# First norm of a two-layer decoder trunk: input read transposed by k-tiles instead of transposed on TensorE

## Chip, cores and metric

The kernel runs on one core of one Trainium2 chip. The metric is the device time of one execution in microseconds (us). Matrix products are made by TensorE (PE in the profile; PEld is its weight load), elementwise work by VectorE (DVE), ScalarE (ACT) and GpSimd (POOL). SyncE (SP) issues most of the loads.

## The reference, cut to what matters

One sequence of 256 tokens with 1024 features goes through two layers (an attention mixer and a SwiGLU block each) and a last norm. The change concerns the norm at the very start and the input projection of the even layer behind it:

```python
def rmsnorm(x, g):
    xf = x.astype(jnp.float32)
    y = xf * lax.rsqrt(jnp.mean(xf * xf, axis=-1, keepdims=True) + NORM_EPS)
    return (y * g.astype(jnp.float32)).astype(x.dtype)
...
    for layer in range(DEPTH):
        j = layer // 2
        h = rmsnorm(x, norm_mix[layer])
        if layer % 2 == 0:
            y = h @ ev_w_in[j]
            qa_nope, qa_rope, c_kv, ka_rope, iq, ik, iw, qb, kb, vb = split_cols(y, EVEN_SPLITS)
...
        x = x + mix
        x = x + swiglu(rmsnorm(x, norm_ffn[layer]), ffn_w_gate[layer], ffn_w_up[layer], ffn_w_down[layer])
    return rmsnorm(x, norm_final)
```

## The kernel before

**Tiling.** The 256 tokens are two tiles `t` of 128. The 1024 features are eight k-tiles of 128 (`KD = 8`). A product contracts over features, so its stationary operand must have features on partitions and tokens along the columns; x lies in memory with tokens first. The kernel therefore transposes x on TensorE: `first_half(nm, t, h)` takes four k-tiles (`h` is the half of the features) of one token tile, multiplies by the identity `ident` into a PSUM bank `pt_x` (L294), and scales by the gain, which is read as a column per k-tile (`gc0`).

**Split into two parts.** Each product is made of three: every operand is split into a high part (`hi`, rounded by a ScalarE copy) and a low part (`lo`, the difference, by VectorE), and `mm3` adds hi x hi, hi x lo and lo x hi (L332, L333, L334). The activations live in one wide tile `aW` (`Norm.wide`) with k-tile, part and token.

**The factor of the norm comes later.** The sum of squares isn't needed for the products. `Norm.square` makes it on ScalarE from natural x, `rsqrt_sum` adds eps on VectorE and raises to the power -0.5 on GpSimd (L226, L227) into `rs[t]`, which multiplies the results of the projection (in `rope`, L392 and after).

**Weights.** The class `Weights` streams all weights in the order of their use: `load` issues a tile (SP queue, L95), `prepare` splits it (`w_hi` on ScalarE, L110; `w_lo` on VectorE, L113), `next` hands it out and prepares six tiles ahead. A tile of the input projection holds two k-tiles of one chunk of columns; the chunks are `EV_CHUNKS` (328, 416, 384, ...), four tiles each. `project` works through one chunk: 4 tiles x 2 k-tiles x 2 token tiles x 3 = 48 products. What this text calls the first chunk has 328 columns, the second 416.

**Order.** The program is written with a tile framework. Its scheduler sets the order of each engine's instructions when the kernel is built, and each engine then runs its list in that order and waits where a semaphore says so. SP's loads and what is marked `pin` keep the order of the code. The start is: seven dummy products (`WARM`, L193) without any input; identity and gain column on ScalarE's queue; halves of x and weight tiles in turns on SP's queue; then the rest of the constants (`con`), `small`, and more weights. `even_mixer` multiplies the first chunk's result by `rs` and the rope tables, transposes it (`pt_i`) and goes on to index scores (`ps_i`). Natural x (`xs`) is needed again at the first residual, at the end of the even mixer.

Of the kernel before, what the change touches and what calls it, by code (L numbers as in the profile page):

```python
# [7 lines left out]
F32 = mybir.dt.float32  # L8
# [7 lines left out]
D = 1024  # L16
# [10 lines left out]
WARM = 7  # L27
# [47 lines left out]
class Weights:  # L75
# [15 lines left out]
    def load(self, upto):  # L91
        while len(self.raw) < min(upto, len(self.queue)):
            src, kk, w = self.queue[len(self.raw)]
            raw = self.spare(len(self.raw)) or self.rpool.tile([P, WCOLS], F32, tag="raw", bufs=self.bufs[0], name="w_raw")
            self.tc.keep_in_program_order(self.tc.nc.sync.dma_start(raw[:, : kk * w], src))  # L95
            self.raw.append(raw)

    def prepare(self, upto, behind=False):

        nc = self.tc.nc  # L100
        while len(self.ready) < min(upto, len(self.queue)):
# [8 lines left out]
            act = nc.scalar.activation(hi[:, :n], raw[:, :n], AF.Copy)  # L110
            if behind:
                self.tc.keep_in_program_order(act)
            nc.vector.tensor_sub(lo[:, :n], raw[:, :n], hi[:, :n])  # L113
# [11 lines left out]
def trunk(tc, x, w0, w1, sm0, cw, vec, gcol, cst, out, dbg=None):  # L125
# [58 lines left out]
    A.dma_start(con[:, :P], cst[:, :P])  # L184
    gc0 = base.tile([P, KD], F32, tag="gc0", name="gc0")
    A.dma_start(gc0, gcol)

# [11 lines left out]
    load_x(0, 0)  # L199
    W.load(1)  # L200
    load_x(1, 0)
    W.load(2)
    load_x(0, 1)
    load_x(1, 1)
    W.load(4)
    pin(nc.sync.dma_start(con[:, P:], cst[:, P:]))
# [83 lines left out]
    def first_half(nm, t, h):  # L290

        pt = t_bank("pt_x").rearrange("p (k c) -> p k c", k=4)
        for i in range(4):
            TE.transpose(pt[:, i], xs[t][:, (4 * h + i) * P : (4 * h + i + 1) * P], ident)  # L294
        hi, lo = nm.aT[t]
        if t == 0 and h == 0:
            for k in range(4):
                g = gc0[:, k : k + 1]
                pin(A.activation(hi[:, k], pt[:, k], AF.Copy, scale=g))
                V.scalar_tensor_tensor(lo[:, k], pt[:, k], g, hi[:, k], op0=ALU.mult, op1=ALU.subtract)  # L300
        else:
            xg = nat("xg").rearrange("p (k c) -> p k c", k=4)
            V.tensor_mul(xg, pt, gc0[:, 4 * h : 4 * h + 4].unsqueeze(2).broadcast_to([P, 4, P]))
            split(hi[:, 4 * h : 4 * h + 4], lo[:, 4 * h : 4 * h + 4], xg)
# [156 lines left out]
    def even_mixer(nm, goff):  # L461
        aT, rs = nm.aT, nm.rs
        with tc.tile_pool(name="even", bufs=1, side="left", reuse_waits="tile") as pool:
# [52 lines left out]
            tc.keep_in_program_order(nc.sync.dma_start(sm, sm0))  # L516
            for t in range(NT):
# [427 lines left out]
    for h in range(2):  # L945
        for t in range(NT):
            first_half(first, t, h)
            W.prepare(2 * h + t + 1, behind=(h,t)==(0,1))
    for t in range(NT):
        for h in range(2):  # L950
            first.square(t, h)
# [135 lines left out]
```

## Time and profile before

| | |
|---|---|
| median of 3 runs | 658.24 us (657.57 to 660.4) |
| profiled execution | 659.6 us |
| its span, first to last instruction | 657.8 us |
| instructions | 10005 |
| PE busy | 643.6 us (98%) |
| VectorE / ScalarE / GpSimd busy | 488.4 / 396.7 / 13.0 us |
| DMA | 109.15 MB, mean 166 GB/s |

Times in the rows are us from the start of the span, where not marked ns. A row of the timeline has start, duration, engine, line, operation, what is written and read, the count, and in brackets idle time ahead of it with what ended it. A row of a group has the count, then the busy time in us, the mean ns of one, and idle time with its releasers. A row of loads has the queue, the count, KB each and the us from issue to landing. PE's rows overlap, since products are pipelined: the distance between two starts is the pace, not the duration.

### The profile page before, as it was taken

The numbers are of one execution on the slowest core, as the hardware profiler recorded it, in microseconds if no ns is written. First come the engines' busy times: TensorE is split into PE (matmuls) and PEld (weight loads), VectorE is DVE, ScalarE is ACT, GpSimd is POOL, SyncE is SP. The second block draws the span as 40 slices with busy tenths as digits, with TensorE's granted clock in tenths as the row PEclk, the third lists the DMA queues.
The fourth block names the chain that finished last, engine by engine and source line by source line (L and its number), as shares of the span: only waits on it lengthen the run. The fifth ranks groups of instructions, "written<-read, shape, count | busy, mean of one in ns | idle before, by whom it ended". The sixth has DMA issues, their size and how long they took to land.

```text
span 657.8 us, 10005 instructions
## 1 busy us (share of the span) xinstructions
PE 643.6 (98%) x3512; PEld 538.5 (82%) x3512; DVE 488.4 (74%) x1115; ACT 396.7 (60%) x800; POOL 13.0 (2%) x26
## 2 busy tenths in 40 slices
PE   8999999999999999999999999999999999999995
PEld 5978888788888888888888877776888888888884
DVE  5999976758977777644579889896698787875424
ACT  5785748548655555433367599695586555554312
POOL 1000000100000000000000000000000000000000
PEclk9999999999999999999999999999999999999999
DMA  8845355138866655664098312410387555555501
GB/s 290 287 138 160 97 166 156 32 111 272 251 193 177 188 184 193 190 192 144 8 344 293 131 65 96 161 65 1 129 271 233 195 184 190 186 190 190 194 25 65
DMA packets 31729, 109.15 MB, mean 166 GB/s; under 512 B 3648, under 2 KB 3904, under 8 KB 31424
## 3 DMA queue, kind: packets, MB, share of 16 engines
q1 hardware_dynamic: 31104, 107.92, 49.6%
q8 instruction: 28, 0.46, 0.3%
q10 hardware_dynamic: 576, 0.59, 0.3%
q14 instruction: 21, 0.17, 0.1%
HBM read 107.46 MB, written 1.05 MB: 165 GB/s over the span
## 4 chain that ended last, share of the span: by engine, by line
PE 84%; ACT 6%; DVE 4%; DMA 4%; issue 2%; POOL 1%; SPq 0%; POOLq 0%; ACTq 0%
PE ps_u L439 12%; PE ps_g L439 11%; PE ps_out L332 7%; PE ps_out L334 7%; PE ps_out L333 7%; PE ps_u L440 6%; PE ps_g L440 6%; PE ps_in L332 5%; PE ps_in L334 5%; PE ps_in L333 5%; DMA w_raw<-in_w 2%; PE ps_o L936 2%; PE pt_p L920 2%; ACT w_hi L110 2%; PE ps_s L901 2%
## 5 line engine op out<-in xcount | busy, mean ns | idle before, releaser
L113 DVE TENSOR_TENSOR w_lo<-w_raw,w_hi 128x1024 fp32r<-128x1024 f32 (+5 forms) x200 | 234.7, 1180 | 93.3 <-ACT w_hi L110 90.9
L110 ACT ACTIVATE w_hi<-w_raw 128x1024 fp32r<-128x1024 f32 (+5 forms) x200 | 203.7, 1023 | 132.1 <-PE ps_out L334 56.8
L439 PE MATMUL ps_u<-aW,w_hi 128*128 128x512 f32 x352 | 124.6, 396 | 0.4 <-DVE hn L452 0.4
L439 PE MATMUL ps_g<-aW,w_hi 128*128 128x512 f32 x352 | 124.5, 395 | 0.3 <-DVE aW L243 0.3
L440 PE MATMUL ps_u<-aW,w_lo 128*128 128x256 f32 x352 | 98.7, 280 | 0.0
L440 PE MATMUL ps_g<-aW,w_lo 128*128 128x256 f32 x352 | 98.7, 280 | 0.0
L439 PEld LDWEIGHTS ps_g<-aW,w_hi 128*128 128x128 f32 x352 | 66.0, 187 | 16.3 <-DVE aW L243 0.9
L439 PEld LDWEIGHTS ps_u<-aW,w_hi 128*128 128x128 f32 x352 | 66.0, 187 | 16.0 <-DVE hn L452 0.7
L332 PE MATMUL ps_in<-w_hi,aW 128*128 128x512 f32 (+5 forms) x208 | 77.3, 372 | 0.6 <-ACT aW L242 0.5
L333 PE MATMUL ps_in<-w_lo,aW 128*128 128x512 f32 (+5 forms) x208 | 77.4, 372 | 0.1
L334 PE MATMUL ps_in<-w_hi,aW 128*128 128x512 f32 (+5 forms) x208 | 75.8, 365 | 0.0
L333 PE MATMUL ps_out<-w_lo,hT_hi 128*128 128x512 f32 x176 | 68.6, 390 | 0.0
L334 PE MATMUL ps_out<-w_hi,hT_lo 128*128 128x512 f32 x176 | 68.6, 390 | 0.0
L332 PE MATMUL ps_out<-w_hi,hT_hi 128*128 128x512 f32 x176 | 68.6, 390 | 0.0
L440 PEld LDWEIGHTS ps_g<-aW,w_lo 128*128 128x128 f32 x352 | 66.5, 189 | 0.0
L440 PEld LDWEIGHTS ps_u<-aW,w_lo 128*128 128x128 f32 x352 | 66.5, 189 | 0.0
L402 ACT ACTIVATE e<-e,bias 128x128 f32<-128x128 f32 (+1 forms) x96 | 42.4, 445 | 2.4 <-DVE bias L401 2.4
L332 PEld LDWEIGHTS ps_in<-w_hi,aW 128*128 128x128 f32 x208 | 39.7, 191 | 5.0 <-ACT aW L242 0.7
L334 PEld LDWEIGHTS ps_in<-w_hi,aW 128*128 128x128 f32 x208 | 39.5, 190 | 4.7 <-issue 0.5
L333 PEld LDWEIGHTS ps_in<-w_lo,aW 128*128 128x128 f32 x208 | 39.5, 190 | 4.4 <-issue 0.5
L334 PEld LDWEIGHTS ps_out<-w_hi,hT_lo 128*128 128x128 f32 x176 | 33.0, 188 | 6.9
L332 PEld LDWEIGHTS ps_out<-w_hi,hT_hi 128*128 128x128 f32 x176 | 33.0, 188 | 6.9
(225 smaller groups left out, 886.6 us busy)
## 6 DMA issues: line engine op xcount, KB each, us to landing
w_raw<-in_w SPq DMA_DIRECT2D x176, 512.0 KB, 4.2
w_raw<-in_w SPq DMA_DIRECT2D x8, 384.0 KB, 4.9
gain<-in_vec SPq DMA_DIRECT2D x4, 512.0 KB, 4.3
cw<-in_cw SPq DMA_DIRECT2D x2, 1024.0 KB, 8.1
w_raw<-in_w SPq DMA_DIRECT2D x4, 416.0 KB, 5.0
w_raw<-in_w SPq DMA_DIRECT2D x4, 328.0 KB, 5.7
w_raw<-in_w SPq DMA_DIRECT2D x4, 304.0 KB, 2.7
x<-in_x SPq DMA_DIRECT2D x4, 256.0 KB, 5.7
```

The source lines that it names most:

```text
L110: act = nc.scalar.activation(hi[:, :n], raw[:, :n], AF.Copy)
L113: nc.vector.tensor_sub(lo[:, :n], raw[:, :n], hi[:, :n])
L332: TE.matmul(ps, act[0][:, k], wh, start=start, stop=False)
L333: TE.matmul(ps, act[0][:, k], wl, start=False, stop=False)
L334: TE.matmul(ps, act[1][:, k], wh, start=False, stop=stop)
L402: A.activation(e, e, AF.Exp, scale=-1.0, bias=bias, accum_out=den)
L439: TE.matmul(dst[f], wh[:, i, c], wide[:, k].rearrange("p z q -> p (z q)"), start=k == 0, stop=False)
L440: TE.matmul(dst[f][:, :T], wl[:, i, c], wide[:, k, 0], start=False, stop=k == KD - 1)
L901: mmi = TE.matmul(sb[:, i], qS[t][:, h], kz[:, par, :, :ns], start=z == 0, stop=z == 1)
L920: TE.transpose(pt[:, i, b, st], e[:, i, b, st * P : (st + 1) * P], ident)
L936: pin(TE.matmul(ob[64 * par : 64 * par + 64], vv[:, st, c : c + 64], pTs[par][:, b, st].rearrange("p j c -> p (j c)"), start=False, stop=l ...
```

## The change

The host passes x a second time, as `xt`: partition p holds, for each k-tile, feature p of it for all 256 tokens. Four tiles `xT` take two k-tiles each. `first_pair` makes the high and low parts straight from them (k-tile by k-tile, 256 tokens wide), so `first_half`, its transposes and the early load of the identity go. The sum over features is now one over partitions: `first_square` squares each `xT` on ScalarE into scratch (the place of natural x, which isn't loaded yet), GpSimd adds the four results, `first_scale` adds the last two halves and sums over partitions by a product with a column of ones, one per token tile (`ps_ms`); eps and power follow as before. The first xT tile and the first weight tile are loaded in two parts each and split in two parts. Natural x is loaded in `even_mixer` behind `sm0`, `con` in one piece behind the first weights, and `WARM` is 9.

```diff
-WARM = 7
+WARM = 9
...
-    def load(self, upto):
+    def load(self, upto, between=None):
...
-            self.tc.keep_in_program_order(self.tc.nc.sync.dma_start(raw[:, : kk * w], src))
+            parts = kk if not self.raw else 1
+            for j in range(parts):
+                c = slice(j * kk * w // parts, (j + 1) * kk * w // parts)
+                self.tc.keep_in_program_order(self.tc.nc.sync.dma_start(raw[:, c], src[:, c]))
+                if between and j == 0:
+                    between()
...
-            act = nc.scalar.activation(hi[:, :n], raw[:, :n], AF.Copy)
-            if behind:
-                self.tc.keep_in_program_order(act)
-            nc.vector.tensor_sub(lo[:, :n], raw[:, :n], hi[:, :n])
+            parts = kk if i == 0 else 1
+            for j in range(parts):
+                c = slice(j * n // parts, (j + 1) * n // parts)
+                nc.scalar.activation(hi[:, c], raw[:, c], AF.Copy)
+                nc.vector.tensor_sub(lo[:, c], raw[:, c], hi[:, c])
...
-    A.dma_start(con[:, :P], cst[:, :P])
     gc0 = base.tile([P, KD], F32, tag="gc0", name="gc0")
     A.dma_start(gc0, gcol)
+    one = base.tile([P, 1], F32, tag="one", name="one")
+    V.memset(one, 1.0)
...
-    load_x(0, 0)
-    W.load(1)
-    load_x(1, 0)
-    W.load(2)
-    load_x(0, 1)
-    load_x(1, 1)
-    W.load(4)
-    pin(nc.sync.dma_start(con[:, P:], cst[:, P:]))
+    xT = [nat("xT") for _ in range(KD // 2)]
+
+    def load_xT(p, i):
+        pin(nc.sync.dma_start(xT[p][:, i.start * T : i.stop * T], xt[:, (2 * p + i.start) * T : (2 * p + i.stop) * T]))
+
+    load_xT(0, slice(0, 1))
+    W.load(1, between=lambda: load_xT(0, slice(1, 2)))
+    for p in range(1, KD // 2):
+        load_xT(p, slice(0, 2))
+        W.load(p + 1)
+    pin(nc.sync.dma_start(con, cst))
...
-    def first_half(nm, t, h):
...
+    def first_pair(nm, p):
+
+        for i in range(2):
+            k = 2 * p + i
+            g = gc0[:, k : k + 1]
+            src = xT[p][:, i * T : (i + 1) * T]
+            A.activation(nm.wide[:, k, 0], src, AF.Copy, scale=g)
+            V.scalar_tensor_tensor(nm.wide[:, k, 1], src, g, nm.wide[:, k, 0], op0=ALU.mult, op1=ALU.subtract)
+
+    sums = xs[1][:, :512]
+
+    def first_square(p):
+
+        dst = sums if p == 0 else xs[0][:, 512 * (p % 2) : 512 * (p % 2) + 512]
+        A.activation(dst, xT[p], AF.Square, scale=1.0 / math.sqrt(D))
+        if p:
+            G.tensor_tensor(sums, sums, dst, op=ALU.add)
+
+    def first_scale(nm):
+
+        G.tensor_tensor(sums[:, :T], sums[:, :T], sums[:, T:], op=ALU.add)
+        pm = t_bank("ps_ms")
+        for t in range(NT):
+            TE.matmul(pm[:, t : t + 1], sums[:, t * P : (t + 1) * P], one, start=True, stop=True)
+        for t in range(NT):
+            V.tensor_scalar(nm.rs[t], pm[:, t : t + 1], EPS, None, op0=ALU.add)
+            G.tensor_tensor(nm.rs[t], nm.rs[t], half_pow[:, :1], op=ALU.pow)
...
             tc.keep_in_program_order(nc.sync.dma_start(sm, sm0))
+            for h in range(2):
+                for t in range(NT):
+                    load_x(t, h)
...
-    for h in range(2):
-        for t in range(NT):
-            first_half(first, t, h)
-            W.prepare(2 * h + t + 1, behind=(h,t)==(0,1))
-    for t in range(NT):
-        for h in range(2):
-            first.square(t, h)
+    for p in range(KD // 2):
+        first_pair(first, p)
+        W.prepare(p + 1)
+        if p:
+            first_square(p - 1)
+    first_square(KD // 2 - 1)
+    first_scale(first)
...
+    xt = x.reshape(T, KD, P).transpose(2, 1, 0).reshape(P, KD * T)
```

What the scheduler makes of it stands in the order of each engine. On TensorE before, from the last dummy product on, transposes of x (`pt_x`) stand among the products of the first chunk (`ps_in_208` and `ps_in_209` are its two token tiles):

```order
L193 MATMUL warm_ps_85<-warm_83 128x512
L294 MATMUL pt_x_110<-con_75,x0_73 128x128 x4
L294 MATMUL pt_x_127<-con_75,x1_74 128x128 x4
L332 MATMUL ps_in_208<-w_hi_123,aW_107 128x328
L333 MATMUL ps_in_208<-w_lo_124,aW_107 128x328
L334 MATMUL ps_in_208<-w_hi_123,aW_107 128x328
```

On TensorE now the dummies are followed directly by products. Near the end of the first chunk (token tiles `ps_in_196` and `ps_in_197`, fourth weight tile `w_hi_152`, `w_lo_153`) the two sum products stand behind the fourth of the twelve products of that tile; the second chunk begins with `ps_in_312` and `ps_in_313`:

```order
L354 MATMUL ps_in_196<-w_hi_152,aW_116 128x328
L355 MATMUL ps_in_196<-w_lo_153,aW_116 128x328
L356 MATMUL ps_in_196<-w_hi_152,aW_116 128x328
L354 MATMUL ps_in_197<-w_hi_152,aW_116 128x328
L323 MATMUL ps_ms_161<-one_82,x1_74 128x1 x2
L355 MATMUL ps_in_197<-w_lo_153,aW_116 128x328
...
L354 MATMUL ps_in_312<-w_hi_200,aW_116 128x416
L354 MATMUL ps_in_313<-w_hi_200,aW_116 128x416
L355 MATMUL ps_in_312<-w_lo_201,aW_116 128x416
```

The transposes are gone from TensorE's list, and eight products of the first chunk now stand behind the sum products. On VectorE before, from the eps of the first norm to the low parts of the second chunk's weight tiles (128x832):

```order
L226 TENSOR_SCALAR rs<-ms_166 128x1
L226 TENSOR_SCALAR rs<-ms_173 128x1
L477 TENSOR_TENSOR lam_p<-small 128x128
L483 TENSOR_SCALAR subg<-small 128x128
L478 TENSOR_REDUCE lam_185<-lam_p 128x2
L243 TENSOR_TENSOR aW<-xg,aW 128x4x128
L392 SCALAR_TENSOR_TENSOR n_294<-ps_in,rs,con 128x320
L481 TENSOR_SCALAR nlam<-lam_185 128x1
L113 TENSOR_TENSOR w_lo<-w_raw,w_hi 128x832 x3
L394 SCALAR_TENSOR_TENSOR rope_b<-ps_in,rs,con 128x5x32
```

and the same place on VectorE now:

```order
L499 TENSOR_TENSOR lam_p<-small 128x128
L325 TENSOR_SCALAR rs<-ps_ms 128x1 x2
L500 TENSOR_REDUCE lam_173<-lam_p 128x2
L505 TENSOR_SCALAR subg<-small 128x128
L414 SCALAR_TENSOR_TENSOR n_282<-ps_in,rs,con 128x320
L503 TENSOR_SCALAR nlam<-lam_173 128x1
L416 SCALAR_TENSOR_TENSOR rope_b<-ps_in,rs,con 128x5x32 x2
L527 TENSOR_SCALAR wv<-ps_in,rs 128x8
L119 TENSOR_TENSOR w_lo<-w_raw,w_hi 128x832
L419 TENSOR_TENSOR n_282<-n_282,rope_b 128x320
```

The two half ropes and `wv` now stand ahead of the first low part of the second chunk, and the next low part comes after the rope's sum; before, three low parts came first. On ScalarE the exponent of lambda (L501, which waits for VectorE's L500) now stands ahead of all four high parts of the second chunk, where before one of them was ahead of it. From the middle of the even layer's input projection on, past the attention scores' first products, the lists of all engines read alike but for the line numbers.

More of the change, by code (lines that the diff above doesn't have):

```diff
@@ L94, in load, with prepare @@
             raw = self.spare(len(self.raw)) or self.rpool.tile([P, WCOLS], F32, tag="raw", bufs=self.bufs[0], name="w_raw")
-            self.tc.keep_in_program_order(self.tc.nc.sync.dma_start(raw[:, : kk * w], src))
+            parts = kk if not self.raw else 1
[4 more added lines that the diff above has]
+                    between()
             self.raw.append(raw)
-    def prepare(self, upto, behind=False):
+    def prepare(self, upto):
         nc = self.tc.nc
@@ L122, in next, with trunk @@
         return got
-def trunk(tc, x, w0, w1, sm0, cw, vec, gcol, cst, out, dbg=None):
+def trunk(tc, x, xt, w0, w1, sm0, cw, vec, gcol, cst, out, dbg=None):
     nc = tc.nc
@@ L288, in square @@
                 rsqrt_sum(self.rs[t], ms)
-    def first_half(nm, t, h):
[L292 to L304, printed above, removed]
+    def first_pair(nm, p):
[19 more added lines that the diff above has]
+            G.tensor_tensor(nm.rs[t], nm.rs[t], half_pow[:, :1], op=ALU.pow)
     class Final:
@@ L1067, in host_layout @@
     gcol = i["norm_mix"][0].reshape(KD, P).T
-    return {"x": i["x"].reshape(T, D), "w0": w0, "w1": w1, "sm0": sm0, "cw": cw, "vec": vec, "gcol": gcol, "cst": constants()}
+    x = i["x"].reshape(T, D)
+    xt = x.reshape(T, KD, P).transpose(2, 1, 0).reshape(P, KD * T)
+    return {"x": x, "xt": xt, "w0": w0, "w1": w1, "sm0": sm0, "cw": cw, "vec": vec, "gcol": gcol, "cst": constants()}
 def kernel(**inputs):
```

## The prediction

> **What bounds the kernel now.** I read the page's chain first (who sets the end), then the windows by stage (span, PE busy, PE weight load, VectorE, ScalarE, GpSimd, clock, DMA share, GB/s), then the timeline of the first 29 us.
>
> ```profile
> PE 84%; ACT 6%; DVE 4%; DMA 4%; issue 2%; POOL 1%; SPq 0%; POOLq 0%; ACTq 0%
> ...
> 7.00:19.00 12.00, 11.49 (x62) 10.38 (x63) 9.87 (x23) 9.75 (x22) 1.60 (x2) 1.00 0.92 323
> 19.00:28.40 9.40, 9.40 (x54) 9.25 (x54) 9.03 (x19) 5.47 (x9) 0.00 (x0) 1.00 0.85 261
> 28.40:46.00 17.60, 17.41 (x91) 13.80 (x90) 16.30 (x51) 15.06 (x31) 1.14 (x2) 1.00 0.65 228
> 46.00:58.00 12.00, 11.97 (x75) 11.51 (x74) 11.83 (x44) 8.15 (x13) 0.00 (x0) 1.00 0.23 66
> 58.00:131.00 73.00, 72.30 (x410) 59.60 (x408) 59.62 (x180) 47.28 (x121) 2.03 (x2) 1.00 0.41 127
> ```
>
> TensorE is the bound: from 19 us to 131 us it idles 0.92 us in all (0 + 0.19 + 0.03 + 0.70). So a lead that TensorE has at 28.4 us lasts to the end if no new wait eats it, and a delay does too. The whole change happens before that point, and the instruction orders of both kernels agree on every engine from the middle of the even layer on. I therefore price one quantity: when TensorE ends the second chunk (416 columns).
>
> ```profile
> 1.22 3.17 PE L193 MATMUL warm_ps<-warm 128*128 128x512 bf16 x7 [1.22 <-DVE warm L190]
> ...
> 7.81 0.62 PE L332 MATMUL ps_in<-w_hi,aW 128*128 128x328 f32 x1
> ...
> 8.51 0.47 PE L334 MATMUL ps_in<-w_hi,aW 128*128 128x328 f32 x1
> ...
> 8.78 0.47 PE L332 MATMUL ps_in<-w_hi,aW 128*128 128x328 f32 x1
> ...
> 12.42 0.31 PE L333 MATMUL ps_in<-w_lo,aW 128*128 128x328 f32 x1
> ...
> 12.57 0.31 PE L334 MATMUL ps_in<-w_hi,aW 128*128 128x328 f32 x1
> ...
> 18.78 0.31 PE L334 MATMUL ps_in<-w_hi,aW 128*128 128x328 f32 x1
> ...
> 18.93 0.35 PE L333 MATMUL ps_in<-w_lo,aW 128*128 128x416 f32 x1
> ...
> 28.25 0.35 PE L334 MATMUL ps_in<-w_hi,aW 128*128 128x416 f32 x1
> 28.43 1.05 PE L548 MATMUL ps_i<-iT 128*128 128x128 f32 x8
> ```
>
> Real products start at 7.81. At 8.5 to 8.8 one of 328 columns takes 0.27 us start to start, at 12.4 to 12.6 it takes 0.15. The first chunk (48 products) is through at 18.93, with one product of the second done early; the other 47, with two groups of transposes, take 9.50 us to 28.43.
>
> **The change, part by part.** *What is removed:* sixteen transposes and their evictions, and the wait of the first transposes for identity and x. That frees the start, so the next limits are the loads, ScalarE and VectorE.
>
> ```profile
> con<-in_cst ACTq DMA_DIRECT2D x1, 64.0 KB, 3.7
> ...
> gc<-in_gcol ACTq DMA_DIRECT2D x1, 4.0 KB, 4.4
> ...
> 4.48 0.81 SPq L95 DMA_DIRECT2D w_raw<-in_w  x2
> ...
> w_raw<-in_w SPq DMA_DIRECT2D x2, 328.0 KB, 5.9
> ...
> 0.74 0.41 ACTq L184 DMA_DIRECT2D con<-in_cst  x1
> ```
>
> *Loads.* The same 1 MB of x (transposed now) and four weight tiles stand ahead of anything else. The fourth tile was issued at about 4.9 (the second of the pair at 4.48) and landed 5.9 later, at 10.8. The 64 KB of identity no longer run ahead, so I take 10.65. The gain column gc0 is now the first load of ScalarE's queue, issued at 0.74 in place of the identity: by the two rows of that queue it lands 3.7 to 4.4 us later, at 4.4 to 5.1; I take 4.6. Every scaled k-tile waits for it.
>
> ```profile
> L242 ACT ACTIVATE stk<-nq 128x256 fp32r<-128x256 f32 x8 | 3.0, 407 | 1.8 <-DVE nq L397 1.8
> L110 ACT ACTIVATE w_hi<-w_raw 128x656 fp32r<-128x656 f32 x4 | 2.9, 743 | 2.8 <-DMA w_raw<-in_w 2.8
> L286 ACT ACTIVATE sq<-x 128x512 bf16<-128x512 f32 x16 | 9.9, 622 | 2.2 <-DVE x L382 1.2 <-DVE x L384 1.0
> L113 DVE TENSOR_TENSOR w_lo<-w_raw,w_hi 128x656 fp32r<-128x656 f32 x4 | 3.3, 834 | 5.1 <-ACT w_hi L110 5.1
> ...
> 16.19 0.89 ACT L110 ACTIVATE w_hi<-w_raw 128x832 fp32r<-128x832 f32 x1
> 16.98 0.19 ACT L479 ACTIVATE lam<-lam 128x2 f32<-128x2 f32 x1
> ```
>
> *ScalarE.* An operation lets the next start 0.10 us before its end (0.89 long, the next 0.79 later). The new queue: eight scaled k-tiles of 256 columns (0.407 - 0.10 = 0.31 each, 2.46), two half weight tiles (between the 256 and the 656 row, 0.37 each, 0.74), three whole ones (0.64 each, 1.93), four squares (0.52 each, 2.09): 7.2 us from 4.6 on, 11.8. Some 0.3 us of waits for landings make it 12.1 for the last square, with the fourth tile's high part done at 11.6. The low parts follow on VectorE 0.83 later: third tile 11.3 (high part 10.4), fourth about 12.8.
>
> *TensorE.* WARM goes from 7 to 9: 9 x 0.43 from 1.22 ends at 5.2, about where the first product becomes ready (5.4), so the two more cost nothing; were that cover gone, 0.9 us. TensorE is fed tile by tile: the twelve products of the third tile run from 11.3 to 13.1, and four of the fourth to 13.7. There the new instruction stands in its queue: two one-column products that collect the sums of squares. They wait for GpSimd, and TensorE's eight last products wait behind them.
>
> *GpSimd,* the unknown price: three 512-wide adds and a 256-wide one; the last two follow the last square.
>
> ```profile
> L223 POOL TENSOR_TENSOR r<-r,half 128x1 f32<-128x1 f32 x2 | 1.1, 569 | 19.2 <-DVE r L222 19.2
> L499 POOL MEMSET kbT<- 64x1024 f32 x2 | 1.9, 947 | 0.1
> ...
> 15.95 1.60 POOL L227 TENSOR_TENSOR rs<-rs,half 128x1 f32<-128x1 f32 x2 [12.56 <-DVE rs L226]
> 27.73 0.49 PE L509 MATMUL pt_i<-con,n 128*128 128x128 f32 x3
> ```
>
> Nothing there is an add of this width. Below: one column costs 0.57 on that engine, so 0.57 each. Above: a fill of 1024 columns moves 1024 elements per partition in 0.95; an add of 512 moves 1536, so 1.42, and 0.71 for the half. I take 0.95 and 0.60, by the fill's row, which is nearest in size. The sums are then ready at S = 12.15 + 0.95 + 0.60 + 0.10 = 13.8; with the low price at 13.7 (TensorE's own arrival), with the high one at 14.4. [...]
>
> *What is late next.* The last eight products end at S + 0.35 + 8 x 0.148 = 15.3: TensorE leads the old kernel by 3.4 us there (18.93 less the 0.19 of the early product). Two products of the second chunk follow; the third needs the low half of the fifth weight tile, and on VectorE that subtraction now stands behind the whole way of the first norm: two additions of eps, the first rope multiply (which waits for GpSimd's power), nlam, two half ropes, wv.
>
> ```profile
> L226 DVE TENSOR_SCALAR rs<-ms 128x1 f32<-128x1 f32 x8 | 1.7, 211 | 0.0
> L392 DVE SCALAR_TENSOR_TENSOR n<-ps_in,rs,con 128x320 f32<-128x320 f32 x2 | 1.1, 546 | 0.0
> L394 DVE SCALAR_TENSOR_TENSOR rope_b<-ps_in,rs,con 128x160 f32<-128x160 f32 x4 | 1.4, 374 | 0.0
> L505 DVE TENSOR_SCALAR wv<-ps_in,rs 128x8 f32<-128x8 f32 x2 | 0.4, 215 | 0.0
> L113 DVE TENSOR_TENSOR w_lo<-w_raw,w_hi 128x832 fp32r<-128x832 f32 x4 | 3.9, 1017 | 0.0
> ```
>
> From S: 0.45 for the two sum products (three transposes take 0.49) and the hand-over, 0.25 to the first eps, 0.80 for the power (1.60 for two) with 0.1 of hand-over: S + 1.6. Then, each 0.08 less than its row, 0.46 + 0.13 + 0.29 + 0.29 + 0.13 = 1.3, and 1.02 for the low part: S + 3.95, and 0.1 to TensorE, S + 4.05 = 17.85. TensorE idles from 15.7 to 17.85. The 46 products left take 9.50 - 0.19 = 9.3: end S + 13.35. **Gain = 28.43 - 13.35 - S = 15.1 - S, at S = 13.8 1.3 us**, 0.7 to 1.4 over the bounds. I keep 1.2, as the chain has one hand-over more on GpSimd.
>
> *Moved loads.* Natural x enters SP's queue behind sm0: four issues of 0.43 and 1.05 MB, at the 323 GB/s of the 7-to-19 row 3.2 us, ahead of weight tiles 14 on. It is needed only at the first residual, after 131 us. Tile 14 is converted later in the new ScalarE order, and in the old run it was ready well ahead of its use:
>
> ```profile
> 23.43 0.43 SPq L516 DMA_DIRECT2D sm<-in_sm  x1
> ...
> 30.81 0.85 ACT L110 ACTIVATE w_hi<-w_raw 128x768 fp32r<-128x768 f32 x1
> ```
>
> Landing 3.2 us later it is there near 33 us, before its turn; cost zero, 2 us if it were not.
>
> *Sum.* The profiled execution took 659.6 us (span 657.8, 1.8 around it). 659.6 - 1.2 = 658.4. The median of the three runs, 658.24, lies 1.4 below that execution, so the forecast for the median is **657.0 us**.
>
> **Rivals.**
> 1. *The lead lasts.* The new orders in 28 to 131 us could remove waits; those are 0.9 us at most, and with S at its low bound the gain is 1.4 + 0.9 = 2.3: 655.9. Against: most of that idle time is in 58 to 131, where the orders hardly change.
> 2. *GpSimd's adds take the place of the wait: slower.* The turning point is S = 15.1. With an add of length a the chain ends at max(8.0 + 2a, 12.2) + 1.5a (the first square ends near 8.0): that is 15.1 at a = 1.9, twice my price. VectorE is busy 9.87 of 12 us in that stretch, much of it with subtractions of two SBUF operands; if the engines slow one another to half speed the gain is nil, and at a = 2.5 S is 16.75, the loss 1.65, the median 659.9. [...] No row of this run has both at work on wide tiles.
> 3. *TensorE stays slow.* The old run kept 0.27 us per product until past 9 us, in spite of 3.2 us of dummies and the transposes, and was fast after three busy microseconds from 7.05. If the feeding by tiles keeps the slow pace through the first chunk, it ends near 19.1, the fifth low part comes at 20.7, and the second chunk ends at 30.1: loss 1.6, or 3 with a slow start of the second chunk too; 659.8 to 661.2. For it: gaps of up to 1 us between tiles. Against: the slow products themselves fill the time from 6 to 10 us. [...]
> 4. *Natural x delays weights:* tile 14 late by 2 us, net loss 0.8: 659.0.
>
> **How the numbers follow.** Forecast (655.9 to 657.8) 0.50; rival 1 0.12; rival 2 0.18; rival 3 0.10; rival 4 0.05; 0.05 for none of these. The range, with a microsecond for the spread that the three runs show (657.57 to 660.4), is 655.0 to 660.3. Half a per cent, 3.3 us, is about what a measurement of this kernel can tell from no change: faster than 654.9 needs the whole 3.4 us lead, chance 0.06; slower than 661.5 needs rival 2 or 3 at its worst, 0.08; within, 0.86.
>
> **What would show it.** Right: the first product near 5.4, the sum products near 13.8, TensorE idle for about 2 us before the third product of the second chunk, its end near 27.2. Wrong: GpSimd adds over 1.9 us, products at 0.27 us after 11 us, or a weight tile awaited from DMA between 28 and 58 us.

## The result, and the profile after

The changed kernel is slower: 666.5 us median of 4 runs (665.67 to 667.64) against 658.38 (657.57 to 660.4), a ratio of 1.012 with a 95% interval of 1.0091 to 1.0149. In a later batch it took 665.91 against 656.6: 1.0141 (1.0119 to 1.0162). The forecast was 657.0.

| | before | after |
|---|---|---|
| profiled execution | 659.6 us | 665.86 us |
| its span | 657.8 us | 663.4 us |
| first real product starts | 7.81 | 4.71 |
| last product of 328 columns starts | 18.78 | 19.60 |
| last product of 416 columns starts | 28.25 | 31.18 |
| GpSimd busy | 13.0 us | 17.5 us |

The page's chain first, then the windows by stage (span; busy time with count of PE, weight load, VectorE, ScalarE, GpSimd; granted clock; DMA share; GB/s):

```profile
PE 84%; DVE 5%; DMA 4%; ACT 4%; issue 2%; POOL 1%; SPq 0%; POOLq 0%; ACTq 0%; DVEq 0%
```

```profile
7.00:19.00 12.00, 9.20 (x41) 8.01 (x41) 8.80 (x15) 6.00 (x12) 5.26 (x5) 0.72 0.89 330
19.00:28.40 9.40, 8.03 (x44) 7.32 (x43) 9.04 (x20) 6.49 (x11) 0.96 (x2) 1.00 0.59 188
28.40:46.00 17.60, 16.97 (x96) 14.64 (x95) 15.15 (x48) 13.55 (x29) 1.10 (x2) 1.00 0.79 285
46.00:58.00 12.00, 11.76 (x61) 10.03 (x61) 11.90 (x46) 8.98 (x13) 0.00 (x0) 1.00 0.42 132
58.00:131.00 73.00, 72.78 (x416) 60.55 (x415) 59.73 (x179) 48.86 (x123) 1.43 (x2) 1.00 0.41 130
```

The chain has the same 84% of TensorE, but VectorE overtook ScalarE in it. From 7 to 19 us TensorE is now busy 9.20 us in place of 11.49, and at a clock of 0.72; from 19 to 28.4 us it idles 1.37 us, where it had idled not at all. GpSimd, with 1.60 us in the first of these windows before, has 5.26. From 58 us on little differs (0.22 idle, 0.70 before). So what is lost up to 131 us is lost before 58 us, and most of it before the second chunk is done. That is about half of the 8 us between the medians; the other half is taken up under "The pace in the SwiGLU blocks".

TensorE's timeline after, in the order of events:

```profile
4.71 0.83 PE L354 MATMUL ps_in<-w_hi,aW 128*128 128x328 f32 x1
...
6.15 0.31 PE L355 MATMUL ps_in<-w_lo,aW 128*128 128x328 f32 x1
6.30 0.31 PE L356 MATMUL ps_in<-w_hi,aW 128*128 128x328 f32 x1
...
7.84 0.31 PE L356 MATMUL ps_in<-w_hi,aW 128*128 128x328 f32 x1
10.39 0.92 PE L354 MATMUL ps_in<-w_hi,aW 128*128 128x328 f32 x2 [2.24 <-ACT w_hi L118]
11.87 0.64 PE L355 MATMUL ps_in<-w_lo,aW 128*128 128x328 f32 x1 [0.56 <-DVE w_lo L119]
12.31 0.48 PE L356 MATMUL ps_in<-w_hi,aW 128*128 128x328 f32 x1
12.58 0.48 PE L355 MATMUL ps_in<-w_lo,aW 128*128 128x328 f32 x1
...
18.11 0.50 PE L323 MATMUL ps_ms<-one,x 128*128 128x1 f32 x4
...
20.14 0.65 PE L354 MATMUL ps_in<-w_hi,aW 128*128 128x416 f32 x2 [0.22 <-ACT w_hi L118]
21.93 0.46 PE L355 MATMUL ps_in<-w_lo,aW 128*128 128x416 f32 x1 [1.15 <-DVE w_lo L119]
```

Three things are to be read from the starts. First, TensorE is at its fast pace early (0.15 us between 6.15 and 6.30), has no work from 8.15 on, and idles 2.24 us. Second, after that idle time the pace is 0.27 us (12.31 to 12.58). Third, it idles again at the second chunk, for the low part of the fifth weight tile. The granted clock in windows of 2 us says the same of the second:

```profile
8.00:10.00 2.00, 0.15 (x2) 0.00 (x0) 0.88 (x2) 1.73 (x4) 0.15 (x1) 0.85 1.03 394
10.00:12.00 2.00, 1.05 (x3) 0.63 (x3) 1.63 (x2) 2.00 (x5) 1.31 (x2) 0.50 1.04 415
12.00:14.00 2.00, 2.00 (x8) 2.00 (x9) 2.00 (x3) 2.00 (x5) 1.35 (x1) 0.50 1.02 387
14.00:16.00 2.00, 2.00 (x9) 2.00 (x9) 2.00 (x3) 0.27 (x1) 1.51 (x1) 0.50 0.99 388
16.00:18.00 2.00, 2.00 (x13) 1.73 (x12) 1.70 (x3) 0.00 (x0) 0.81 (x1) 0.94 0.60 210
```

By the shares of the first and the last window, half clock from about 9.4 to 16.2 us, 6.8 us.

Where the idle time comes from: the chain of waits (start, duration, what) and ScalarE's timeline beside it.

```profile
2.59 5.65 DMA xT<-in_xt
```

```profile
8.27 0.91 ACT L306 ACTIVATE aW<-xT,gc 128x256 fp32r<-128x256 f32 x2 [1.57 <-DMA xT<-in_xt]
9.08 0.62 ACT L314 ACTIVATE x<-xT 128x512 f32<-128x512 f32 x1
9.60 0.74 ACT L118 ACTIVATE w_hi<-w_raw 128x656 fp32r<-128x656 f32 x1
```

The second xT tile lands at 8.24. Then ScalarE makes two high parts, squares the tile, and only then converts the second weight tile, for which TensorE waits.

GpSimd's adds, and VectorE beside them:

```profile
9.85 1.27 POOL L316 TENSOR_TENSOR x<-x,x 128x512 f32<-128x512 f32 x1 [6.48 <-ACT x L314]
11.80 1.55 POOL L316 TENSOR_TENSOR x<-x,x 128x512 f32<-128x512 f32 x1 [0.69 <-ACT x L314]
14.41 1.51 POOL L316 TENSOR_TENSOR x<-x,x 128x512 f32<-128x512 f32 x1 [1.06 <-ACT x L314]
16.00 0.81 POOL L320 TENSOR_TENSOR x<-x 128x256 f32<-128x256 f32 x1
```

```profile
8.81 0.88 DVE L307 SCALAR_TENSOR_TENSOR aW<-xT,gc,aW 128x256 fp32r<-128x256 f32 x2 [1.58 <-ACT aW L306]
10.37 1.44 DVE L119 TENSOR_TENSOR w_lo<-w_raw,w_hi 128x656 fp32r<-128x656 f32 x1 [0.68 <-ACT w_hi L118]
11.74 1.90 DVE L307 SCALAR_TENSOR_TENSOR aW<-xT,gc,aW 128x256 fp32r<-128x256 f32 x2
13.56 0.83 DVE L119 TENSOR_TENSOR w_lo<-w_raw,w_hi 128x656 fp32r<-128x656 f32 x1
14.31 1.90 DVE L307 SCALAR_TENSOR_TENSOR aW<-xT,gc,aW 128x256 fp32r<-128x256 f32 x2
16.13 1.37 DVE L119 TENSOR_TENSOR w_lo<-w_raw,w_hi 128x656 fp32r<-128x656 f32 x1
```

The same VectorE work takes 0.88 or 1.90 us, 0.83 or 1.37 to 1.44: long whenever an add runs. The subtraction that starts at 10.37 ends 0.69 after the first add (11.81 against 11.12), the one at 16.13 ends 0.69 after the last (17.50 against 16.81). The second product of each pair of 1.90 lasts 1.50 us and ends 0.29 after the add that runs beside it (13.64 against 13.35, 16.21 against 15.92). In these rows that reads as a wait for the add's end, not as a slowing by a share; what the two engines contend for isn't shown.

### The profile page after: what moved, and what is told of

Same layout as the page of the kernel before. It is cut to its first block, busy times and chain, and to the rows that moved or that the text cites. A ratio compares the mean times of both kernels' runs of the same rounds, so it can differ in the third digit from the quotient of the medians.

```text
span 663.4 us, 9988 instructions
## 1 busy us (share of the span) xinstructions
PE 646.6 (97%) x3502; PEld 538.6 (81%) x3502; DVE 490.3 (74%) x1115; ACT 397.6 (60%) x798; POOL 17.5 (3%) x30
## 4 chain that ended last, share of the span: by engine, by line
PE 84%; DVE 5%; DMA 4%; ACT 4%; issue 2%; POOL 1%; SPq 0%; POOLq 0%; ACTq 0%; DVEq 0%
PE ps_u L461 12%; PE ps_g L461 11%; PE ps_out L354 7%; PE ps_out L356 7%; PE ps_out L355 7%; PE ps_u L462 6%; PE ps_g L462 6%; PE ps_in L355 5%; PE ps_in L356 5%; PE ps_in L354 5%; DMA w_raw<-in_w 3%; DVE w_lo L119 2%; PE ps_o L961 2%; PE pt_p L945 2%; PE ps_s L926 1%
## 5 line engine op out<-in xcount | busy, mean ns | idle before, releaser
L119 DVE TENSOR_TENSOR w_lo<-w_raw,w_hi 128x1024 fp32r<-128x1024 f32 (+6 forms) x201 | 236.4, 1181 | 93.2 <-ACT w_hi L118 90.6
L118 ACT ACTIVATE w_hi<-w_raw 128x1024 fp32r<-128x1024 f32 (+6 forms) x201 | 204.2, 1020 | 126.4 <-PE ps_out L356 56.7
L354 PE MATMUL ps_in<-w_hi,aW 128*128 128x512 f32 (+5 forms) x208 | 78.0, 378 | 2.6 <-ACT w_hi L118 2.5
L356 PE MATMUL ps_in<-w_hi,aW 128*128 128x512 f32 (+5 forms) x208 | 76.9, 370 | 0.0
L355 PEld LDWEIGHTS ps_out<-w_lo,hT_hi 128*128 128x128 f32 x176 | 33.0, 188 | 6.8
```

What stands on the lines that cost most here:

```text
L118: nc.scalar.activation(hi[:, c], raw[:, c], AF.Copy)
L119: nc.vector.tensor_sub(lo[:, c], raw[:, c], hi[:, c])
L354: TE.matmul(ps, act[0][:, k], wh, start=start, stop=False)
L355: TE.matmul(ps, act[0][:, k], wl, start=False, stop=False)
L356: TE.matmul(ps, act[1][:, k], wh, start=False, stop=stop)
```

## The experiments

All start from the changed kernel and change one thing in its code, but for those that say otherwise; where the scheduler then put other instructions in another place too, the text says so. The offset that some texts name is worked out from the timelines: the same ScalarE instructions are matched with the first profile of before, and the median difference of their starts is taken in a stretch.

| run | last 416-column product | offset 100–140 us | median, runs | ratio to before (95%) |
|---|---|---|---|---|
| before (first profile; again) | 28.25; 27.52 | 0; -0.91 | | |
| after (first profile; again) | 31.18; 30.75 | +4.07; +2.80 | 666.5; 665.91 | 1.012; 1.0141 |
| first tiles whole | 30.12 | +4.07 | 663.45, 10 | 1.0066 (1.0043–1.0088) |
| no adds | 29.32 | +2.38 | 664.3, 5 | 1.0079 (1.004–1.0118) |
| fifth low part first | 28.92 | +2.29 | 664.69, 6 | 1.0087 (1.0058–1.0117) |
| 34 dummies | 31.00 | +3.74 | 665.89, 4 | 1.0095 (1.006–1.0129) |
| natural x late | 30.75 | +3.38 | 665.45, 4 | 1.0116 (1.0086–1.0147) |
| old sums, natural x early | 28.71 | +0.79 | 662.6, 4 | 1.0071 (1.0045–1.0097) |
| all remedies | 24.95 | -2.58 | 659.29, 12 | 1.0022 (1.0004–1.004) |
| all remedies, no tile of ones | 25.16 | -3.43 | 657.51, 12 | 0.9982 (0.9959–1.0005) |

**Parts of the change undone, one at a time.** The first xT tile and the first weight tile in one piece:

```diff
-            parts = kk if not self.raw else 1
+            parts = 1
...
-            parts = kk if i == 0 else 1
+            parts = 1
...
-    load_xT(0, slice(0, 1))
-    W.load(1, between=lambda: load_xT(0, slice(1, 2)))
+    load_xT(0, slice(0, 2))
+    W.load(1)
```

> The first xT tile and the first weight tile are loaded and split whole, as the other tiles are; all else as changed. Mark: the start of the first index-score product, which is the end of the second chunk (31.37 us in the changed kernel, 28.43 before). Theory 'small transfers': the halves (1 KB and 1.3 KB per partition) make the loads slow, and the second xT tile landed at 8.24 for that; whole, it lands by 7.2, ScalarE and VectorE follow 1 us earlier, TensorE's idle time of 2.24 us ahead of the second tile shrinks below 1 us, the mark comes at 30.4 and the span is about 1 us shorter than 663.4. Rival 'the loads are slow for another reason': the second xT tile lands at 8.0 to 8.4 as before, TensorE only starts later, and the mark stays within 0.4 us of 31.4.

The first product started at 7.21, 2.5 us later, and yet the second chunk's last product came 1.06 earlier (30.12). ScalarE took up the second xT tile at 7.06 without a wait, where it had waited until 8.27. So the early start was paid for by the next tile. Half clock came all the same, from about 7.9 to 11.3, with 2.28 us of idle time ahead of the first product. In this profile the lead was given back by 100 us; it was taken of an execution of 665.08 us, though, and the median of the ten is 663.45.

The adds stand elsewhere here, and the subtractions beside them last 1.51 (from 9.15) and 1.94 us (from 11.38). Both end 0.70 us behind the add that was running (10.66 against 9.96, 13.32 against 12.62): the length varies, the distance to the add's end doesn't.

GpSimd's three adds of 512 left out (so the sum of squares lacks three quarters of the features):

```diff
         A.activation(dst, xT[p], AF.Square, scale=1.0 / math.sqrt(D))
-        if p:
-            G.tensor_tensor(sums, sums, dst, op=ALU.add)
```

> The three 512-wide additions of squares on GpSimd are left out, so the factor of the first norm comes from the first quarter of the features only; the order of the first chunk's products on TensorE and the place of the sum products are held by hand as in the changed kernel. Theory 'GpSimd slows VectorE': without the adds the scaled low parts of 256 columns take 0.45 to 0.5 us each and not 0.95, the subtraction of 656 columns 0.83 and not 1.4, and the low part of the fourth weight tile is ready by 15.2 and not at 17.5. If that alone set the end of the first chunk, the mark (start of the first index-score product, 31.37 in the changed kernel) comes at 29.0. Rival 'TensorE at half rate sets it': the low parts are early, but products at 0.27 us until past 15 us end the first chunk at 19 or later, and the mark is at 30.6 or later. If the low parts are as slow as with the adds, the theory falls.

VectorE's timeline in this run, the counterpart of the rows above:

```profile
10.05 0.84 DVE L119 TENSOR_TENSOR w_lo<-w_raw,w_hi 128x656 fp32r<-128x656 f32 x1 [0.67 <-ACT w_hi L118]
...
13.07 0.88 DVE L307 SCALAR_TENSOR_TENSOR aW<-xT,gc,aW 128x256 fp32r<-128x256 f32 x2
13.87 0.84 DVE L119 TENSOR_TENSOR w_lo<-w_raw,w_hi 128x656 fp32r<-128x656 f32 x1
```

Every one is at its short time, and the fourth tile's low part is done at 14.7, not 17.5. That the adds made them long is thereby shown. TensorE gained 1.9 us only, since it was at half clock until 13.8 and then stood 1.64 us before the fifth low part. How much of the 1.9 is the adds' alone isn't shown: against what was written ahead of it, the edit doesn't hold TensorE's order, and in this kernel the two sum products stand thirteen products earlier (at 14.30, in the third tile), and the exponent of lambda and the fifth high part behind it (15.87 in place of 19.20) are earlier too.

The fifth low part ahead of the norm's eps on VectorE:

```diff
+                sub = nc.vector.tensor_sub(lo[:, c], raw[:, c], hi[:, c])
+                if i == 4:
+                    self.tc.keep_in_program_order(sub)
...
-            V.tensor_scalar(nm.rs[t], pm[:, t : t + 1], EPS, None, op0=ALU.add)
+            pin(V.tensor_scalar(nm.rs[t], pm[:, t : t + 1], EPS, None, op0=ALU.add))
...
+    W.prepare(5)
     first_scale(first)
```

> On VectorE the low part of the first tile of the second chunk is held by hand ahead of the eps of the first norm, and so ahead of the rope; nothing else is added or removed. Theory 'the low part behind the rope costs its wait': TensorE's idle time of 1.37 us at the start of the second chunk (20.1 to 21.9) falls under 0.4 us and the mark comes 1.0 to 1.4 us earlier, at 30.0 to 30.4. Rival 'it is given back': the rope starts later, the transposes of the first chunk's result wait for it, and the mark stays at 31.1 to 31.5.

The third product of the second chunk, now without a wait:

```profile
19.86 0.46 PE L357 MATMUL ps_in<-w_lo,aW 128*128 128x416 f32 x1
```

The idle time before the third product of the second chunk is gone (it starts at 19.86, not 21.93), and the last one comes at 28.92: 2.3 us gained, more than either theory gave. One more thing moved: lambda's reduction now also stands ahead of the eps on VectorE (17.45, not 18.78), so ScalarE comes to the fifth high part at 17.87, not 19.20. The gain is that of both.

Dummies until the data are there:

```diff
-WARM = 9
+WARM = 34
```

> 34 dummy products instead of 9, so that TensorE is busy without a break until about 10.2 us, when the second weight tile is ready; the order of the first chunk's products is held by hand; the scheduler also puts two low parts of the second chunk ahead of the eps. Theory 'clock': the gap at 8.0 to 10.4 us made the products of 328 columns go back to 0.27 us; without it they take 0.15 throughout, and the first chunk ends as soon as the operands allow. Theory 'GpSimd slows VectorE' then sets that: the fourth low part is at 17.5 as before, the first chunk ends at 19.3, and the mark (31.37 in the changed kernel) is at 29.0 to 29.4 because the low part no longer stands behind the rope. If the clock alone had been the limit, the first chunk ends at 17.6 and the mark is at 27.6. If products still take 0.27 us, the clock theory falls and the mark is past 31.

TensorE's longest wait in the second chunk now:

```profile
26.71 0.55 PE L538 MATMUL pt_i<-con,n 128*128 128x128 f32 x3 [1.52 <-DVE n L535]
```

The clock stays at 1.00 and products run at 0.15 from 11.6 on, but the last one of 328 columns starts at 19.25, near the 19.3 that the theory of the adds said. The dummies hold the first product until 11.24, and TensorE, fast now, still comes to the fourth tile about 0.2 us ahead of its low part (done at 17.14). In the changed kernel TensorE, at half clock until 16.2, waits for that low part too (17.39 to 17.56). So half clock alone cost nothing here; it lay beside VectorE's delay. The gain that was expected in the second chunk went to a wait of 1.52 for the rope's result, since two low parts now stand ahead of the eps. Its last product, at 31.00, is within the spread of the changed kernel itself (31.18 and 30.75).

**Natural x, and the old way of summing.** First only the four loads of x, moved behind the projection chunks:

> Only the four loads of natural x move, from behind sm0 to behind the projection chunks of the even mixer (some 30 us later). Everything up to the end of the second chunk stays, so the last product of 416 columns starts near 31.2 as in the changed kernel. Theory A (what is lost between 31 and 60 us, 1.1 us of the 4.1, comes from the scheduler's order on VectorE, which puts the low parts of tiles 12 and 13 ahead of the second chunk's ropes): tile 13 was issued ahead of x already, the order stays, TensorE still waits for n at the first pt_c, and ScalarE's times between 100 and 140 us lie 3.5 to 4.2 us behind the kernel before. Theory B (the loads of natural x slow the weight tiles beside them, tile 13's 5.3 us above all): tile 13 lands within 4.2 us of its issue, the wait at pt_c goes, and the offset at 100 to 140 us falls to 2.9 to 3.1. Time: A 665.5 to 667, B 664.8 to 665.8.

Neither theory held as put. Tile 13 needed 5.53 us to land without x beside it (5.28 with it), so x isn't what slows it. The wait at pt_c stayed (0.82), and the offset of 3.38 lies between the two profiles of the changed kernel itself (4.07 and 2.80). x costs nothing that this can tell.

Then the transposed input with the old sums: squares and sums from natural x as before, loaded behind the fifth weight tile, with low parts and ropes held in turns on VectorE (the lines here leave that out):

```diff
-        if p:
-            first_square(p - 1)
-    first_square(KD // 2 - 1)
-    first_scale(first)
+    W.prepare(5)
+    for t in range(NT):
+        for h in range(2):
+            first.square(t, h)
...
+    W.load(5)
+    for t in range(NT):
+        for h in range(2):
+            load_x(t, h)
     pin(nc.sync.dma_start(con, cst))
```

> The transposed input alone: the sums of squares are made as in the kernel before, from natural x, which is loaded behind the fifth weight tile; no GpSimd adds and no sum products. The low parts of tiles 4 to 8 and the first ropes are held in turns on VectorE, so that no low part stands behind both ropes. Theory A (the loss up to the second chunk is GpSimd's adds, which slow VectorE, and the fifth low part behind the ropes; the slow TensorE after its idle time costs the rest): low parts of 656 columns take 0.84 us, the fourth is done near 14.7, the last 328-column product starts at 17.4 to 17.9, the second chunk runs without an idle time over 0.3 us, and its last product starts at 26.8 to 27.5 (before 28.25, after 31.18). Time 656.8 to 658.8, offset at 100 to 140 us -1.5 to 0. Theory B (natural x, one megabyte ahead of tiles 5 and after, only changes places with the lost time: weight tiles come late): TensorE waits for high parts of tiles 5 to 7, the last product starts at 28.3 to 29.5, time 658.5 to 660.5. Theory C (feeding TensorE tile by tile is itself the loss): the last 328-column product still starts at 19 or later.

The first chunk agrees with the theory of the adds (last product at 17.49), the second with its rival: short waits for high and low parts and a last product at 28.71. Natural x ahead of the weights gives part of the gain back: the sixth weight tile is converted only when it lands, at 19.29. The time, 662.6, lies over both theories' ranges; what is missing is not in the first 131 us, where the offset is 0.79. In this profile 2.3 us more are lost in the second SwiGLU block.

**All remedies together.** Whole first tiles, 16 dummies, low parts and ropes in turns on VectorE, and the sums of (bf16) squares by TensorE:

```diff
-WARM = 9
+WARM = 16
...
+            for k in range(KD):
+                pin(TE.matmul(pm[:, t : t + 1], sqT[:, k * T + t * P : k * T + (t + 1) * P], one, start=k == 0, stop=k == KD - 1))
...
+    W.load(6)
     pin(nc.sync.dma_start(con, cst))
...
+            W.ahead = 2
             ps = project(aT, EV_CHUNKS[0], nm)
+            W.ahead = 4
...
+                W.prepare(8 + t)
```

> A version meant to beat both: first xT tile and first weight tile whole, 16 dummies, squares of xT in bf16 summed over features by 16 one-column products on TensorE instead of GpSimd's adds, constants behind the sixth weight tile, low parts of tiles 4 to 8 and first ropes in turns on VectorE. If the causes named so far (slow TensorE after an idle time, VectorE slowed by GpSimd, fifth low part behind the ropes) are all there is: first product at 7.2 to 7.5, products at 0.15 us from the start, low parts of 656 columns in 0.84, last 328-column product at 14.3 to 15.8, the second chunk's last product at 24.3 to 25.6 (before 28.25), and 654.5 to 656.5 if the lead lasts, 656.5 to 658.5 if later waits in 28 to 60 us eat it. If the start is bound by something else (weight tiles landing later than they do beside fewer loads): the last 328-column product at 16.5 or later and 657.5 to 660.

The last products start at 15.07 and 24.95, inside the expected ranges: with the causes of the single runs undone together, the start has gained 6.2 us on the changed kernel, all that it had lost and 3.3 us of lead over the first profile of before, 2.6 over its second. No product runs at half clock. As this version also loads the constants later and prepares weights in another order, it doesn't tell the shares of the causes apart. The time, 659.29, lies over the forecast all the same: some 7 us under the changed kernel, but 0.2% over before. In its profile the lead of 2.58 us at 130 us has become a lag of 0.47 at 600; 2.3 us of it go between 480 and 590, in the second SwiGLU block. This led to the next runs.

**The pace in the SwiGLU blocks.** There TensorE works without a gap on pairs of a 512- and a 256-column product, and a pair takes 0.347 or 0.353 us from start to start, the same all through a block: 2.2 us a block. Both paces stand in windows of 20 us, by the count of products, first of before:

```profile
220.00:240.00 20.00, 20.00 (x115) 17.35 (x114) 15.76 (x26) 11.73 (x22) 0.00 (x0) 1.00 0.59 189
500.00:520.00 20.00, 20.00 (x117) 17.65 (x116) 15.71 (x27) 12.02 (x23) 0.00 (x0) 1.00 0.64 203
```

and of the first profile of the changed kernel:

```profile
220.00:240.00 20.00, 20.00 (x115) 17.31 (x114) 15.39 (x25) 11.74 (x22) 0.00 (x0) 1.00 0.62 188
500.00:520.00 20.00, 20.00 (x115) 17.33 (x114) 16.20 (x26) 11.88 (x22) 0.00 (x0) 1.00 0.63 213
```

> The kernel before, unchanged, profiled once more. If the pace of the products in the two SwiGLU blocks (0.347 or 0.353 us for a pair of 512 and 256 columns) is a matter of the single execution, this profile can show either pace in either block, and up to 28 us its rows agree with the first profile within 0.1 us. If the pace belongs to the program, it shows 0.353 in the first block and 0.347 in the second, as the first profile did.

The same two windows of this run:

```profile
220.00:240.00 20.00, 20.00 (x117) 17.62 (x117) 16.13 (x26) 11.40 (x21) 0.00 (x0) 1.00 0.63 194
500.00:520.00 20.00, 20.00 (x117) 17.47 (x117) 16.14 (x26) 11.50 (x21) 0.00 (x0) 1.00 0.56 194
```

Before again ran at 0.347 in both blocks, in a profiled execution of 655.99 us. So the pace is not fixed by the program. Its start didn't agree with the first profile within 0.1: the second group of transposes waits for x until 6.30 there, not 7.05, and the second chunk's last product starts at 27.52, not 28.25. The first profile of before had a late start itself.

Two runs put one suspect each into the kernel before: the tile of ones, and the additional input.

> The kernel before with one thing of the change alone: the column of ones, a new tile of four bytes per partition in the base pool, with its fill (not used further). No engine's order changes; what moves is the place in SBUF of what is allocated after it. Theory P (the slower pace of the SwiGLU products, 0.353 us a pair in place of 0.347, which all profiles of kernels with the change show in the second block and one of two profiles of before shows in the first, comes from the shifted places): the second block's products run at 0.353, and the median is 2 to 4.5 us over the kernel before. Theory R (the pace is chance, or comes from elsewhere): median within 0.8 us of before, and paces of 0.347 appear.

> The kernel before with the transposed copy of x handed over as one more input that nothing reads: no order changes and nothing moves in SBUF; the other inputs can lie elsewhere in device memory. Theory D (the slower pace comes from where the weights lie in memory): 0.353 in the second block, median 2 to 4.5 us over before. Otherwise: median within 0.8 us of before.

With the tile: 0.353 in both blocks, 660.64 against 658.57, ratio 1.0022 (1.0 to 1.0043); none of its 12 executions took under 658.88, where 17 of the 28 of before did. With the input: 0.347, then 0.353, 658.84, ratio 1.0 (0.9975 to 1.0026). The first hinted at the place in SBUF, so two more took the tile out, of the version with all remedies and of the changed kernel (these lines are of the second; the other puts the column into the other tile of natural x):

```diff
-    one = base.tile([P, 1], F32, tag="one", name="one")
-    V.memset(one, 1.0)
...
+    one = xs[1][:, 512:513]
+    V.memset(one, 1.0)
```

> The version with all remedies, without the tile of ones in the base pool: the column of ones lies in the place of natural x until that is loaded, so every later tile stands where it stands in the kernel before. Theory P: the second block's products are back at 0.347 (often the first block's too), and the lead of 2.6 us that this version showed from 90 us on lasts: median 2 to 4 us below the version with the tile of ones, 1.5 to 3.5 us below the kernel before. Theory R or D: no difference to the version with the tile of ones, 0.5 to 2.5 us over the kernel before.

> The changed kernel, but the column of ones lies in a free part of natural x's place instead of a tile of its own in the base pool, so every later tile stands in SBUF where it stands in the kernel before; the order of the engines is that of the changed kernel. Theory P (the four bytes move later tiles, and that brings the slow executions): median 1.4 to 3 us below the changed kernel run beside it, and some executions are faster than any of its. Theory R (chance): within 0.8 us of it.

> The changed kernel itself, again, beside the others on one chip: its median 665.7 to 667.2, the rows up to 31 us within 0.2 us of the first profile's (last product of the second chunk at 31.0 to 31.4). The pace in the SwiGLU blocks: 0.353 in both by theory P, either pace by theory R.

All remedies without the tile: 657.51, 1.8 us below the version with it (of another batch; against the before of its own batch each, 0.4% apart) and 1.1 below before, with an interval that holds no change (0.9959 to 1.0005); its profile ran at 0.353 in both blocks nevertheless. The changed kernel without the tile: 664.98, beside 665.91 with it; a difference of 0.9 that the spread of either (3 us) covers. Its profile ran at 0.353, then 0.347; that of the changed kernel again at 0.347, then 0.353, and its second chunk ended earlier than expected (30.75). So the place of four bytes is not shown to set the pace; that it has a part in the time isn't excluded. Counting profiled blocks, kernels that read the transposed input ran at 0.347 in 4 of 24, kernels with the old start in 4 of 8. Whether the start has a hand in it stays open.

**31 to 60 us.** The second chunk's ropes ahead of the low parts of tiles 12 and 13:

```diff
+            W.ahead = 4
             ps = project(aT, EV_CHUNKS[1])
+            W.ahead = 6
```

> The changed kernel, but while the second chunk runs weights are prepared only four tiles ahead, so that on VectorE the ropes of the second chunk stand ahead of the low parts of tiles 12 and 13. Up to the last product of the second chunk (31.2 us) nothing changes. Theory A (those low parts, which wait for a weight tile, hold the ropes and so TensorE): the wait for n at the first pt_c is at most 0.3 us, and the offset of ScalarE's times at 100 to 140 us falls from 4.07 to 2.8 to 3.3; time 665 to 665.8. Theory B (the 1.1 us come from elsewhere between 31 and 60 us): offset 3.7 to 4.3, time 666 to 667.

TensorE's wait at pt_c, in the changed kernel and in this one:

```profile
35.42 0.41 PE L557 MATMUL pt_c<-con,n 128*128 128x128 f32 x2 [0.57 <-DVE n L419]
```

```profile
33.19 0.41 PE L559 MATMUL pt_c<-con,n 128*128 128x128 f32 x2 [0.35 <-DVE n L419]
```

The wait shrank to 0.35, just outside what the theory allowed, but the offset stayed at 3.9: theory A falls as the cause of the whole 1.1 us. The time, 665.71, lies in its range, but 0.2 below the changed kernel beside it is nothing that can be told. The second profile of the changed kernel, in the old order, had no wait there and only 0.3 us lost between the second chunk and 100 us. How much goes there may depend on when tile 13 lands in the single execution; that isn't settled.

## Why the prediction was wrong

Its last product of 416 columns was to start 1.2 us earlier than before; it started 2.9 us later (3.2 by the second profiles). By its own steps:

- **What bounds the kernel** was right: TensorE is the bound, and what is lost by 31 us is still lost at 131 (offset 4.07).
- **Loads: right for the start, wrong for the next tile.** The gain column was there at 3.75 (4.6 predicted), the first product started at 4.71 (5.4). But the step asked only when the fourth weight tile lands, and allowed "some 0.3 us of waits for landings". The second xT tile landed at 8.24 and ScalarE stood 1.57 us for it, behind 0.65 us for the second part of the first weight tile (0.69 and 1.14 in the second profile). With the first tiles whole it was taken up at 7.06.
- **TensorE's pace: the step that "the slow products themselves fill the time from 6 to 10 us" failed.** TensorE was fast at 6 us, had nothing from 8.15 on, and with the idle time of 2.24 us it went to half clock for nearly 7 us; with 34 dummies and no idle time it stayed at 1.00. This is the third rival, with 0.10 the least likely but one, which had thought of gaps "of up to 1 us". The stretches at half clock lasted about 3.4 us (no adds; changed kernel again) or 6.8 (first profile); what sets their length isn't shown.
- **ScalarE and VectorE: "fourth about 12.8" was 17.5, the largest miss.** Of the 4.7 us, 2.8 are the adds' (14.7 without them); the rest goes mostly with the late second tile, behind which all others queue. The row that the step used, 0.83 for a low part, was right for an undisturbed VectorE. The second rival let the two engines disturb one another, but charged that to the adds ("if the engines slow one another"), not to the subtractions, for which TensorE waits. So its turning point, adds of 1.9 us, was never reached, and the loss came with adds of 1.3 to 1.55.
- **GpSimd's adds** took 1.27 to 1.55 us in place of 0.95, the small one 0.81 in place of 0.60; the upper bound, 1.42, was broken too. The sums were ready at 16.8, not 13.8, but nobody waited for them: TensorE came to the sum products at 18.11. The price of the add hardly mattered as such, what it held up did.
- **"S + 4.05"** was right as a chain: with 18.1 for S it gives 22.15 for the third product, which started at 21.93. The fifth low part behind the ropes was named as what is late next; at a TensorE that comes late too, it cost 1.15 us of idle time, and putting it first gained 2.3.
- **Dummies at no cost, natural x at no cost:** borne out (products follow the dummies at once; x late gains nothing that can be told).
- **The rivals were priced one at a time.** Two came true together, 2.9 us later by the second chunk, where the forecast had let each of them cost it 1.6 to 3 us alone. By the last product of the second chunk the single remedies gained 1.1, 1.9, 2.3 and 0.2 us (the last within the spread of two profiles), all together 6.2: a remedy alone only moved the wait to the next cause.
- **From 3 to 4 us at the start to 8 in the time.** The first profiles differ by 5.6 us of span: an offset of 4.07 by 131 us, 0.6 less by 470, and 2.3 more in the second SwiGLU block. The second profiles differ by 7.6: 3.7 by 131 us, 0.3 in the first block, 1.5 around 335 us (TensorE waits 2.06 us ahead of `pt_f` in the second layer, 0.20 in before), 2.3 in the second block. The prediction let a lead or a delay at 28 us last to the end, as the lists agree downstream; an execution's pace there is worth 2.2 us a block, and the text knew of the spread only as a microsecond. What happens behind 131 us isn't explained: chance of a single execution alone doesn't fit a version that leads by 2.6 us there and whose 12 executions have a median over that of before.

## What to carry to other kernels

Where an engine is fed piece by piece, price each piece's arrival, not the last one's: an early start that runs dry can end later than a late one (31.18 against 30.12 here). Before moving work to GpSimd, look at what VectorE does in that stretch: in these rows subtractions and products of two SBUF operands ended only 0.69 to 0.70 and 0.29 us after the GpSimd add beside them, and the engine behind VectorE paid. And where several causes lie beside one another, undo them together as well as singly; here no single remedy gained half of what all did at the end of the second chunk.

## What was not expected of the hardware

- A VectorE subtraction of 656 columns, with two SBUF operands, ended 0.69 to 0.70 us after the end of the GpSimd add that ran when it started, twice in the changed kernel and twice with whole first tiles; 0.84 became 1.37 to 1.94, a pair of 0.88 became 1.90 to 2.38.
- An idle time of 2.24 us was followed by half clock for about 6.8 us, in other executions of the same kernel's start (idle 1.36, with 0.95 and 0.92 beside it) for about 3.4. When the stretch begins differs too: 9.4 in the first profile, 10.4 without the adds, 12.0 in the changed kernel again. The clock column shows these phases; of the slow pace at the start of the kernel before (0.27 us between 8.51 and 8.78) it shows nothing (1.00).
- Products in the SwiGLU blocks ran at one of two paces, 0.347 or 0.353 us a pair, 1.7% apart, for a whole block, and which one varied between executions of one kernel (before: 0.353, then 0.347; again: 0.347 in both). The cause was not found.
